# Adaptive-norm products of layer 0 on VectorE, mLSTM projections ahead of the state weights, and other tiles for layer 1's chunks

## The chip, the core and the metric

The kernel runs on one core of a Trainium2 chip. The metric is the device time of one execution in microseconds (us). Engines go by the profile's names: PE is TensorE (matmuls; PEld is its weight load), DVE is VectorE, ACT is ScalarE, POOL is GpSimd, SP is SyncE, whose queue issues the loads.

## What is computed

Two layers of a diffusion trunk over 256 latent and 256 context tokens, width 1024, float32. For this change three pieces of the reference matter.

```python
s_c, s_cc = jax.nn.silu(c), jax.nn.silu(c_ctx)
mod   = jnp.split((s_c @ w_ada[l] + b_ada[l])[:, None, :], 6, axis=-1)
mod_c = jnp.split(s_cc @ w_ada[l][:, :n_cm * D_MODEL] + b_ada[l][:n_cm * D_MODEL], n_cm)   # n_cm: 6 in layer 0, 2 in layer 1
h = modulate(rms_norm(x, g_norm1[l]), mod[0], mod[1])                # then h @ w_in[l] for four parallel mixers
# mixer B (mLSTM): q and k are silu(short_conv(h @ w_bq)), silu(short_conv(h @ w_bk));
# its stabiliser is a running sum and a running maximum over the tokens of the gate projections
x = x + mod[2] * (merge_branches(ya, yb, yc, yd) @ w_out[l])
x = x + mod[5] * squared_relu_mlp(modulate(rms_norm(x, g_norm2[l]), mod[3], mod[4]), w_ff1[l], w_ff2[l])
```

The modulation is a product of one row (or two rows, with the context's) with a 1024 x 6144 matrix: 24 MB a layer are read for very little arithmetic.

## The kernel before, in words

All weights are streamed once. A piece of weight is 128 x 1024 floats (512 KB): `_prep` loads it into a `raw` tile (three of these go round), ScalarE rounds it to `whi` (L136), VectorE takes the remainder `wlo` (L137), and a product is three TensorE passes over the high and low parts (L164 to L166, L193 to L195, L215 to L217). There are two `whi` and two `wlo` tiles, apart from some pieces that are kept longer, which take the four wide `w8` tiles (`wide`). The order of the pieces is a list, `specs`, made by the plan functions; `get` hands out the next piece and lets `_prep` run one piece ahead. Below this list a scheduler orders each engine's instructions by their place in the program and by when it reckons them ready; on the chip each engine then runs its list in order.

Between the pieces lie the chunks of the modulation matrix (`ada`): `plan` puts one behind each split piece while the list `fill` lasts. A chunk isn't split. Its load goes into a `raw` tile too, and right after the `get` of the piece before it `ada_chunk` uses it. Layer 0's first third of the matrix is done by another path at the start (`ada_start`, L529). Its other two thirds are 32 chunks (two groups g of 16, each of 8 rows k by two halves j), which follow the pieces of mixer A, its readout (RA), mixer B and the first merges (M0). For each of them TensorE runs four matmuls of 256 columns (L400) into the four 32-row bands of a PSUM tile that it holds through a whole group, with both conditioning vectors as the stationary operand; `ada_end` then copies, transposes and adds the bias.

Layer 1's 48 chunks (g 0 to 2) lie between the pieces of layer 0's feed-forward. These go to VectorE (`ada_vec`): each chunk is multiplied by a per-partition scalar and added to a 128 x 1024 accumulator in a `w4` tile (L360 for the first row, L362 for the others), once for each side, where group 0 has two sides (latent and context) and the others one. After eight chunks `ada_sum` adds the accumulator over the partitions with matmuls against a selector (L374), four for each side.

Mixer B (`mixer_b`): the gate projection (L215 to L217), its transpose, then on VectorE a chain of logarithm, running sums and running maxima on 36 rows (L783 to L817), which ends in a small diagonal matrix (`bdg`, L821). TensorE multiplies it with ones (L823), transposes U, and then projects k and q (four pieces, `bk`, `bq`, by `fm`, L164 to L166), each followed by a short convolution (`conv`, L749 to L757), and then v (`bv`, four pieces). State weights (L855) follow the projection of v.

Of the kernel before, what the change touches and what calls it, by code (L numbers as in the profile page):

```python
# [10 lines left out]
AF = mybir.ActivationFunctionType  # L11
ALU = mybir.AluOpType
# [5 lines left out]
TOK = CTX + LAT  # L18
KT = DM // 128
# [12 lines left out]
P_BADA, P_G1, P_G2 = 0, 96, 112  # L32
# [8 lines left out]
class Trunk:  # L41
# [63 lines left out]
    def _prep(self):  # L105
        nc = self.nc
        i = self.next_prep
        self.next_prep += 1
        key, parts, split, dest = self.specs[i]
        if key[0] == "ad" and key[1]:  # L110
            raw = self.t("w4", [128, 1024])
        else:
            raw = self.wp.tile([128, 1024], F32, name=f"raw{i}", tag="raw", bufs=self.wb)
# [226 lines left out]
    def ada_specs(self, l, g):  # L340
        w = self.io["w_ada"]
        out = []
        for k in range(KT):
            for j in range(2):
                c0 = g * 2048 + j * 1024
                out.append((("ada", l, g, k, j), [(w[l, k * 128:(k + 1) * 128, c0:c0 + 1024].rearrange("p (a c) -> p a c", a=1), (1, 1024))], False, None))
        return sorted(out, key=lambda o: o[0][4]) if l else out

    def ada_vec(self, key):

        nc = self.nc
        _, l, g, k, jj = key
        raw, _ = self.get(key)
        sides = (0, 1) if g == 0 else (0,)
        if k == 0:
            self.ada_acc = [self.t("w4", [128, 1024], name=f"aacc{g}{jj}{r}") for r in sides]
        for r in sides:
            acc, s = self.ada_acc[r], self.scol[:, k, r:r + 1]
# [30 lines left out]

    def ada_chunk(self, key):  # L390
        nc = self.nc
        _, l, g, k, jj = key
        if l:
            return self.ada_vec(key)
        raw, _ = self.get(key)
        if k == 0 and jj == 0:
            self.ada_ps = self.pd()
        for q in range(4):

            nc.tensor.matmul(self.ada_ps[32 * q:32 * q + 32, jj * 256:(jj + 1) * 256], self.scol[:, k, :], raw[:, q * 256:(q + 1) * 256],  # L400
                             start=(k == 0 and jj == 0), stop=(k == KT - 1), skip_group_check=True)
        if k == KT - 1 and jj == 1:
            self.ada_end(l, g, self.ada_ps)

    def ada_end(self, l, g, ps):
        nc = self.nc
        row = self.t("d2", [128, 512], name=f"arow{l}{g}")
        nc.scalar.activation(out=row, in_=ps, func=AF.Copy)
        pt = self.pm()
        for c in range(4):  # L410
            self.tr(pt[:, c * 128:(c + 1) * 128], row[:, c * 128:(c + 1) * 128])
        n0 = l * 48 + g * 16
        view = lambda ap: ap.rearrange("p (j q c) -> p j c q", j=2, q=4)
        bias = view(self.PT[:, P_BADA + n0:P_BADA + n0 + 16])
        for r in range(2):
            for jj in range(2):
                nc.vector.tensor_tensor(
                    out=view(self.MOD[l][:, g * 16:(g + 1) * 16, r])[:, jj],
                    in0=pt.rearrange("p (j c q s) -> p j c q s", j=2, c=2, q=4)[:, jj, :, :, r],
                    in1=bias[:, jj], op=ALU.add)  # L420
        self.ada_gs(l, g, (0, 1))
# [338 lines left out]
    def mixer_b(self, l):  # L760
# [59 lines left out]
        for a in range(2):  # L820
            nc.vector.tensor_scalar(out=dg[0:R, a, :], in0=self.ident[0:R, 0:R], scalar1=me[0:R, a:a + 1], scalar2=None, op0=ALU.mult)  # L821
        pe = self.pm()
# [15 lines left out]
        kT = [self.conv(l, 1, mt, self.fm(self.get(("bk", l, mt)), 0, TOK), 0, 0.125) for mt in range(2)]  # L838
        qT = [self.conv(l, 0, mt, self.fm(self.get(("bq", l, mt)), q0, TOK), q0, 1.0) for mt in range(2)]
# [698 lines left out]
```

## Time and profile before

| | us |
|---|---|
| median of 3 runs | 1850.93 (1849.62 to 1853.4) |
| the profiled execution, its own time | 1851.94 |
| span of its profile | 1850.2 |
| PE busy in it | 1805.8 (98%) |
| DVE busy | 1134.1 (61%) |
| ACT busy | 836.3 (45%) |
| granted TensorE clock, mean | 0.994 |

The profile is of one execution. Busy time is summed per engine over its instructions; a wait is the idle time of an engine just before an instruction, put down to what that instruction waited for last. A window row gives the busy time of each engine in a stretch, with the number of instructions in brackets, then the granted TensorE clock as a share of 2.4 GHz. Of TensorE, matmuls are pipelined: the distance from one start to the next tells the cost of one, not the duration that is shown.

### The profile page before, as it was taken

How to read it: one execution, taken by the hardware profiler on the slowest of the kernel's cores; microseconds unless marked ns; L12 is line 12 of the kernel's file. 1: busy time of each engine (PE TensorE's matmuls, PEld its weight loads, DVE VectorE, ACT ScalarE, POOL GpSimd, SP SyncE). 2: the span in 40 equal slices, each digit the busy share in tenths (PEclk: the TensorE clock that was granted, in tenths of full speed). 3: DMA queues.
4: the chain of work that ended last, by engine and by line, in shares of the span. 5: the costliest groups of instructions: out<-in, count | busy, mean ns of one | idle time of the engine just before them, and what ended most of it. 6: DMA issues, size and time to landing. Idle time of an engine off the chain costs nothing.

```text
span 1850.2 us, 28703 instructions
## 1 busy us (share of the span) xinstructions
PE 1805.8 (98%) x11414; PEld 1554.8 (84%) x11414; DVE 1134.1 (61%) x1983; ACT 836.3 (45%) x1487; POOL 123.1 (7%) x139
## 2 busy tenths in 40 slices
PE   7999999999999999999999999999999999989998
PEld 5888877799667778898777888988899979889998
DVE  5566654627754444557775665588665866566665
ACT  4343433434763333443333334444454774545555
POOL 0000000000001111010111000000000001001110
PEclk9999999999999999999999999999999999999999
DMA  9533343333112233315565655222234524544554
GB/s 288 180 92 100 117 149 117 112 109 91 46 35 69 68 126 114 114 45 159 164 192 179 192 183 159 72 69 69 81 118 150 160 68 138 159 149 148 183 183 137
DMA packets 222343, 235.26 MB, mean 127 GB/s; under 512 B 8320, under 2 KB 209408, under 8 KB 221952
## 3 DMA queue, kind: packets, MB, share of 16 engines
q1 hardware_dynamic: 222208, 233.42, 40.9%
q8 instruction: 90, 1.47, 0.3%
q14 instruction: 45, 0.37, 0.1%
HBM read 229.20 MB, written 4.19 MB: 126 GB/s over the span
## 4 chain that ended last, share of the span: by engine, by line
PE 81%; DVE 7%; DMA 6%; ACT 3%; issue 2%; SPq 0%; POOL 0%; ACTq 0%; DVEq 0%; POOLq 0%
PE pd L193 12%; PE pd L195 12%; PE pd L194 12%; DMA raw<-in_w_ada_dram 5%; PE pd L215 5%; PE pd L216 4%; PE pd L217 4%; PE pd L164 4%; PE pd L165 4%; PE pd L166 4%; PE pm L642 2%; PE pm L233 2%; DVE wlo L137 2%; PE pm L909 1%; PE pm L1100 1%
## 5 line engine op out<-in xcount | busy, mean ns | idle before, releaser
L137 DVE TENSOR_TENSOR wlo<-raw,whi 128x1024 fp32r<-128x1024 f32 x305 | 386.3, 1267 | 299.1 <-ACT whi L136 297.2
L136 ACT ACTIVATE whi<-raw 128x1024 fp32r<-128x1024 f32 x305 | 322.0, 1057 | 402.2 <-PE pd L194 171.8
L195 PE MATMUL pd<-HH,wlo 128*128 128x256 f32 (+1 forms) x1104 | 371.7, 337 | 8.8 <-DVE wlo L137 8.7
L193 PE MATMUL pd<-HH,whi 128*128 128x256 f32 (+1 forms) x1104 | 372.9, 338 | 1.2 <-ACT whi L136 1.2
L194 PE MATMUL pd<-HL,whi 128*128 128x256 f32 (+1 forms) x1104 | 371.5, 337 | 0.0
L195 PEld LDWEIGHTS pd<-HH,wlo 128*128 128x128 f32 x1104 | 210.0, 190 | 32.0 <-DVE wlo L137 11.8
L193 PEld LDWEIGHTS pd<-HH,whi 128*128 128x128 f32 x1104 | 209.9, 190 | 25.9 <-issue 3.9
L194 PEld LDWEIGHTS pd<-HL,whi 128*128 128x128 f32 x1104 | 209.9, 190 | 20.8 <-issue 0.7
L193 PE MATMUL pd<-b,whi 128*128 128x256 f32 (+1 forms) x528 | 175.5, 332 | 0.0
L195 PE MATMUL pd<-b,wlo 128*128 128x256 f32 (+1 forms) x528 | 175.2, 332 | 0.2 <-DVE wlo L137 0.2
L194 PE MATMUL pd<-b,whi 128*128 128x256 f32 (+1 forms) x528 | 175.3, 332 | 0.0
L215 PE MATMUL pd<-whi,HH 128*128 128x256 f32 x592 | 169.0, 286 | 0.0
L217 PE MATMUL pd<-wlo,HH 128*128 128x256 f32 x592 | 168.6, 285 | 0.0
L216 PE MATMUL pd<-whi,HL 128*128 128x256 f32 x592 | 168.0, 284 | 0.0
L215 PEld LDWEIGHTS pd<-whi,HH 128*128 128x128 f32 x592 | 113.4, 192 | 4.2 <-issue 4.1
L216 PEld LDWEIGHTS pd<-whi,HL 128*128 128x128 f32 x592 | 113.4, 192 | 0.3 <-issue 0.2
L217 PEld LDWEIGHTS pd<-wlo,HH 128*128 128x128 f32 x592 | 113.4, 192 | 0.2 <-issue 0.2
L362 DVE SCALAR_TENSOR_TENSOR aacc<-raw,scol,aacc 128x1024 f32<-128x1024 f32 x56 | 72.9, 1308 | 59.4 <-DMA raw<-in_w_ada_dram 59.2
L193 PEld LDWEIGHTS pd<-b,whi 128*128 128x128 f32 x528 | 100.3, 190 | 10.5 <-issue 0.8
L195 PEld LDWEIGHTS pd<-b,wlo 128*128 128x128 f32 x528 | 100.3, 190 | 10.2 <-DVE wlo L137 0.9
L194 PEld LDWEIGHTS pd<-b,whi 128*128 128x128 f32 x528 | 100.3, 190 | 9.3
L437 ACT ACTIVATE w<-X 128x256 f32<-128x256 f32 x120 | 48.1, 413 | 128.9 <-DVE X L1257 128.9
(419 smaller groups left out, 3312.3 us busy)
## 6 DMA issues: line engine op xcount, KB each, us to landing
raw<-in_w_in_dram SPq DMA_DIRECT2D x148, 512.0 KB, 3.5
raw<-in_w_ff_dram SPq DMA_DIRECT2D x128, 512.0 KB, 3.9
raw<-in_w_ada_dram SPq DMA_DIRECT2D x80, 512.0 KB, 4.0
raw<-in_w_branch_dram SPq DMA_DIRECT2D x24, 512.0 KB, 3.4
raw<-in_w_out_dram SPq DMA_DIRECT2D x16, 512.0 KB, 3.4
w<-in_w_ada_dram SPq DMA_DIRECT2D x28, 256.0 KB, 5.5
raw<-in_w_branch_dram SPq DMA_DIRECT2D x16, 256.0 KB, 4.0
spill<-X SPq DMA_DIRECT2D x1, 2048.0 KB, 8.6
```

Source lines behind the costliest of these rows:

```text
L136: nc.scalar.activation(out=hi[:, 0:n], in_=raw[:, 0:n], func=AF.Copy)
L137: nc.vector.tensor_tensor(out=lo[:, 0:n], in0=raw[:, 0:n], in1=hi[:, 0:n].bitcast(F32), op=ALU.subtract)
L164: nc.tensor.matmul(out, lh, rh, start=(i == 0), stop=False)
L165: nc.tensor.matmul(out, lh, rl, start=False, stop=False)
L166: nc.tensor.matmul(out, ll, rh, start=False, stop=(i == n - 1))
L193: nc.tensor.matmul(o, wh, act[0], start=(k == 0), stop=False, skip_group_check=True)
L194: nc.tensor.matmul(o, wh, act[1], start=False, stop=False, skip_group_check=True)
L195: nc.tensor.matmul(o, wl, act[0], start=False, stop=(k == KT - 1), skip_group_check=True)
L215: nc.tensor.matmul(o, hh, wh, start=first, stop=False, skip_group_check=True)
L216: nc.tensor.matmul(o, hl, wh, start=False, stop=False, skip_group_check=True)
L217: nc.tensor.matmul(o, hh, wl, start=False, stop=last, skip_group_check=True)
L362: nc.vector.scalar_tensor_tensor(out=acc, in0=raw, scalar=s, in1=acc, op0=ALU.mult, op1=ALU.add)
```

## The change

Three things are changed.

1. Layer 0's 32 chunks go the way of layer 1's: VectorE multiplies and accumulates, for both sides, and `ada_sum` closes each half group; the TensorE path with `ada_end` is gone. The chunks of layer 0 are sorted by half, as layer 1's are.
2. In both layers, mixer B's four projections of k and q with their convolutions stand before the matmul L823 in the program.
3. The chunks of layer 1 are loaded into `w8` tiles (four, the size of two chunks each) and no longer into `raw` tiles.

```diff
@@ _prep
         if key[0] == "ad" and key[1]:
             raw = self.t("w4", [128, 1024])
+        elif key[0] == "ada" and key[1]:
+            raw = self.t("w8", [128, 1024])
         else:
             raw = self.wp.tile([128, 1024], F32, name=f"raw{i}", tag="raw", bufs=self.wb)
@@ ada_specs
-        return sorted(out, key=lambda o: o[0][4]) if l else out
+        return sorted(out, key=lambda o: o[0][4])
-    def ada_vec(self, key):
+    def ada_chunk(self, key):
         nc = self.nc
         _, l, g, k, jj = key
         raw, _ = self.get(key)
-        sides = (0, 1) if g == 0 else (0,)
+        sides = (0, 1) if l == 0 or g == 0 else (0,)
...
-    def ada_chunk(self, key):
-        nc = self.nc
-        _, l, g, k, jj = key
-        if l:
-            return self.ada_vec(key)
-        raw, _ = self.get(key)
-        if k == 0 and jj == 0:
-            self.ada_ps = self.pd()
-        for q in range(4):
-            nc.tensor.matmul(self.ada_ps[32 * q:32 * q + 32, jj * 256:(jj + 1) * 256], self.scol[:, k, :], raw[:, q * 256:(q + 1) * 256],
-                             start=(k == 0 and jj == 0), stop=(k == KT - 1), skip_group_check=True)
-        if k == KT - 1 and jj == 1:
-            self.ada_end(l, g, self.ada_ps)
-    def ada_end(self, l, g, ps):
...
@@ mixer_b
             nc.vector.tensor_scalar(out=dg[0:R, a, :], ...)
+        kT = [self.conv(l, 1, mt, self.fm(self.get(("bk", l, mt)), 0, TOK), 0, 0.125) for mt in range(2)]
+        qT = [self.conv(l, 0, mt, self.fm(self.get(("bq", l, mt)), q0, TOK), q0, 1.0) for mt in range(2)]
         pe = self.pm()
         nc.tensor.matmul(pe[:, 0:72], self.ones[0:R, :], dg[0:R].rearrange("p a b -> p (a b)"), start=True, stop=True)
...
         nc.scalar.activation(out=wk, in_=wk, func=AF.Exp)
-        kT = [self.conv(l, 1, mt, self.fm(self.get(("bk", l, mt)), 0, TOK), 0, 0.125) for mt in range(2)]
-        qT = [self.conv(l, 0, mt, self.fm(self.get(("bq", l, mt)), q0, TOK), q0, 1.0) for mt in range(2)]
         V = self.t("w8", [128, 4, 4, 129], name=f"bv{l}")
```

## Rows read from the trace of the kernel before

**Rows 1.** The page's first part: busy time, share and instructions of each engine.
```profile
PE 1805.8 (98%) x11414; PEld 1554.8 (84%) x11414; DVE 1134.1 (61%) x1983; ACT 836.3 (45%) x1487; POOL 123.1 (7%) x139
```
**Rows 2.** Windows of layer 0's chunk stretch (length; busy PE, PEld, DVE, ACT, POOL; clock; DMA).
```profile
72.00:205.00 133.00, 132.57 (x889) 109.18 (x888) 89.47 (x149) 51.96 (x83) 1.64 (x4) 1.00 0.32 96
205.00:286.00 81.00, 78.60 (x580) 65.58 (x580) 48.81 (x82) 35.78 (x53) 0.53 (x1) 1.00 0.47 145
286.00:364.00 78.00, 78.00 (x449) 58.58 (x446) 42.91 (x114) 30.60 (x71) 2.44 (x8) 1.00 0.34 107
```
**Rows 3.** Waits of PE from 840 to 1135 us, then of the span (total, times, longest).
```profile
PE pd L195 <- DVE wlo L137: 8.0, 6, 3.1
...
PE pm L823 <- DVE bdg L821: 5.9, 2, 3.5
```
**Rows 4.** Timeline of PE around one chunk of layer 0 (start, duration, engine, line).
```profile
104.69 0.39 PE L165 MATMUL pd<-HL,whi 128*128 128x512 f32 x1
104.92 0.40 PE L166 MATMUL pd<-HH,wlo 128*128 128x512 f32 x1
105.24 0.64 PE L400 MATMUL pd<-raw,scol 128*32 128x256 f32 x8
105.81 0.50 PE L164 MATMUL pd<-HH,whi 128*128 128x512 f32 x1
106.15 0.39 PE L165 MATMUL pd<-HL,whi 128*128 128x512 f32 x1
```
**Rows 5.** The same windows as rows 2, L400 alone (busy PE, PEld with counts).
```profile
72.00:205.00 133.00, 10.12 (x96) 2.41 (x96) 1.00 0.32 96
205.00:286.00 81.00, 8.89 (x96) 2.15 (x96) 1.00 0.47 145
286.00:364.00 78.00, 5.11 (x64) 1.26 (x64) 1.00 0.34 107
```
**Rows 6.** Timeline of PE around one sum of layer 1, two sides.
```profile
893.61 0.39 PE L195 MATMUL pd<-HH,wlo 128*128 128x512 f32 x1
893.93 1.07 PE L374 MATMUL pm<-aacc,selr 128*32 128x256 f32 x16
894.93 0.50 PE L193 MATMUL pd<-HH,whi 128*128 128x512 f32 x1
```
**Rows 7.** Lines L360 and L362 (minimum/median/maximum ns), and L362's group on the page.
```profile
L360 DVE TENSOR_SCALAR aacc<-raw,scol x8: 748/752/754, 833.7 to 1071.1; 128x1024 f32<-128x1024 f32 x8
L362 DVE SCALAR_TENSOR_TENSOR aacc<-raw,scol,aacc x56: 1271/1285/1916, 840.8 to 1111.8; 128x1024 f32<-128x1024 f32 x56
L362 DVE SCALAR_TENSOR_TENSOR aacc<-raw,scol,aacc 128x1024 f32<-128x1024 f32 x56 | 72.9, 1308 | 59.4 <-DMA raw<-in_w_ada_dram 59.2
```
**Rows 8.** Windows: a head of layer 1's mixer A, and the feed-forward of layer 0.
```profile
1206.00:1228.00 22.00, 22.00 (x129) 18.16 (x128) 18.69 (x41) 10.41 (x19) 0.00 (x0) 1.00 0.30 85
840.00:865.00 25.00, 25.00 (x112) 20.71 (x111) 20.26 (x24) 8.51 (x13) 1.49 (x1) 1.00 0.52 155
```
**Rows 9.** Waits of DVE in 840 to 865 us (total, times, longest).
```profile
DVE aacc L362 <- DMA raw<-in_w_ada_dram: 3.0, 3, 1.4
```
**Rows 10.** Windows of mixer B in layer 1, and line L855.
```profile
1307.00:1311.00 4.00, 0.54 (x3) 0.19 (x2) 3.71 (x11) 0.47 (x1) 0.00 (x0) 0.87 0.41 130
1311.00:1317.00 6.00, 6.00 (x27) 5.67 (x27) 3.88 (x6) 4.38 (x8) 0.00 (x0) 0.52 0.19 59
...
L855 DVE TENSOR_TENSOR w<-pm,bwk x8: 414/416/425, 283.7 to 1345.3; 128x256 f32<-128x256 f32 x8
```
**Rows 11.** Timelines of DVE and PE in the feed-forward at 912 us.
```profile
912.52 1.28 DVE L362 SCALAR_TENSOR_TENSOR aacc<-raw,scol,aacc 128x1024 f32<-128x1024 f32 x1 [3.85 <-DMA raw<-in_w_ada_dram]
913.73 1.22 DVE L137 TENSOR_TENSOR wlo<-raw,whi 128x1024 fp32r<-128x1024 f32 x1
...
915.00 0.50 PE L195 MATMUL pd<-HH,wlo 128*128 128x512 f32 x1 [2.30 <-DVE wlo L137]
```
**Rows 12.** Window behind the longest stall of the feed-forward.
```profile
1006.00:1010.00 4.00, 4.00 (x12) 3.09 (x11) 1.23 (x2) 0.26 (x1) 0.00 (x0) 0.57 0.97 332
```

More of the change, by code (lines that the diff above doesn't have):

```diff
@@ L388, in ada_sum @@
                 self.ada_gs(l, g, sides)
-    def ada_chunk(self, key):
-        nc = self.nc
-        _, l, g, k, jj = key
-        if l:
-            return self.ada_vec(key)
-        raw, _ = self.get(key)
-        if k == 0 and jj == 0:
-            self.ada_ps = self.pd()
-        for q in range(4):
-            nc.tensor.matmul(self.ada_ps[32 * q:32 * q + 32, jj * 256:(jj + 1) * 256], self.scol[:, k, :], raw[:, q * 256:(q + 1) * 256],
-                             start=(k == 0 and jj == 0), stop=(k == KT - 1), skip_group_check=True)
-        if k == KT - 1 and jj == 1:
-            self.ada_end(l, g, self.ada_ps)
-    def ada_end(self, l, g, ps):
[L406 to L421, printed above, removed]
     def ada_gs(self, l, g, sides):
```

## The prediction

> **What bounds the kernel now.** I read the engines' totals first [rows 1]: TensorE is busy for 98% of the span, VectorE for 61%. So time can be won only where TensorE does less or waits less, and lost only where it waits more. The windows come next [rows 2]. In the stretch with layer 0's chunks (72 to 364 us) TensorE is busy for 289.2 of 292 us, while VectorE's busy time by windows is 89.47, 48.81 and 42.91, in all 181.2 us. The reader is to see that TensorE sets the pace there and that VectorE has room, but not the same room in each window. Then the waits [rows 3]: TensorE stands 8.0 us for the low parts of weights (`wlo`) in layer 0's feed-forward, 6 times, and 5.9 us for `bdg` in mixer B, twice in the span. Each part of the change touches one of these: TensorE's work in 72 to 364 us, the wait of L823, and the wait for `wlo` in the feed-forward.
>
> **Part 1, layer 0's chunks: what goes.** From one matmul of 512 columns to the next lie 0.23 us, start to start (104.69 to 104.92 [rows 4]). Around a chunk it is 0.32 ahead of L400, 0.57 for its four matmuls (eight records), and 0.34 behind. Less the two distances of 0.23 that are there anyway, a chunk costs 0.09 + 0.57 + 0.11 = 0.77 us. The records per window are 96, 96 and 64 [rows 5], so 12, 12 and 8 chunks, and TensorE loses 32 x 0.77 = 24.6 us of work.
>
> A page prices this otherwise: by the Trainium skill, FP8 and Floating Point Precision, TensorE Precision Notes, true float32 takes four passes; as an estimate from that and 2.4 GHz, four matmuls of 256 columns would be 1.7 us and the 32 chunks 55 us. The row has 0.57 us for the four, which lie in four separate bands of 32 columns, and the row decides.
>
> **What comes.** Four sums, one after each eight chunks, each as the two-sided one of layer 1 [rows 6]: 1.00 us and the same 0.2 around it, 4.8 us (one of them in the first window, two in the second, one in the third). The transposes stay eight; in four groups where there were two they add two such switches, 0.4 us, left to the range. TensorE's balance is -19.8 us. On VectorE each chunk is two instructions: 8 of 64 at 0.752 us and 56 at 1.285 us [rows 7], 78.0 us, 2.44 us a chunk. Loads are the same in number and size on SP's queue. What changes there is when a `raw` tile comes free: so far after TensorE's 0.57 us, then after VectorE's two instructions, and a load of the next piece waits behind that on SP.
>
> **Where VectorE stops hiding it.** With the chunks its busy time is 89.5 + 29.3 = 118.8 in the first window (133 us), 48.8 + 29.3 = 78.1 in the second (81 us) and 42.9 + 19.5 = 62.4 in the third (78 us). TensorE alone would need 133 - 9.2 + 1.2 = 125.0, 81 - 9.2 + 2.4 - 2.4 = 71.8 (with part 2's wait gone) and 78 - 6.2 + 1.2 = 73.0. So VectorE becomes the limit in the first two windows unless it can be kept busy without a break. How far it can be is nowhere shown for this mixture. Two rows bound it [rows 8]: a head of layer 1's mixer A, a chain through three engines, has it busy for 18.69 of 22.00 us, 0.85, with TensorE full; and 840 to 865 us, chunks among other work, for 20.26 of 25 us of which 3.0 went on chunk loads [rows 9], so 0.92 of the time that was left, with TensorE at 25.00 of 25.00. I take 0.92, since a chunk's instructions wait for their load alone and can lie in the gaps of the chains, as they do in that row. Then the windows become 118.8/0.92 = 129.1 (-3.9), 78.1/0.92 = 84.9 (+3.9) and 73.0 (-5.0, TensorE still the limit): -5 us. I give back 1 us for chunk loads that come late as in the feed-forward (59.2 us of waits there over 56 instructions [rows 7], but with 48 chunks from 833.7 to 1111.8 us, 5.8 apart; here they are 81/12 = 6.8 to 133/12 = 11 apart). Part 1 with the first wait of part 2: **-4 us**. Its ends: 0.85 throughout gives 139.8, 91.9 and 73.4, that is +13; TensorE the limit throughout gives 125.0 + 71.8 + 73.0 = 269.8, that is -22.
>
> **Part 2, mixer B.** L823 waits 3.5 us in layer 1 and, by the difference, 2.4 in layer 0 [rows 3]. In layer 0 that is inside the second window and counted above. In layer 1 the wait has a tail: 1307 to 1311 us has 0.54 us of matmuls, and 1311 to 1317 us runs at a granted clock of 0.52 [rows 10], the lower level of 1.2 GHz, so about 2.9 of these 6 us are lost. Together 6.4. After the change the four projections stand ahead of L823 and cover the chain: two of them already ran ahead of it, the other two bring 48 matmuls more. What queues behind: L823, the transposes of U, and the weights up to L855, which runs until 1345.3 in layer 1, 34 us behind the end of the wait; four v pieces lie between, so they can be some 6 us later for nothing. On VectorE the remainders of the two q pieces now fall into the scan chain (1.22 us each), and the convolutions come behind it, so the first PSUM tile for v may be late by about 1 us. I take **-5 us**; the ends are -6.4, and +3 if TensorE waits for a q piece's `wlo` about as long as it waited for `bdg`.
>
> **Part 3, the feed-forward.** One stall shows them all [rows 11]: VectorE stands 3.85 us before a chunk's instruction for its load, the `wlo` behind it is late, and TensorE waits. A load can only be issued when one of three `raw` tiles, shared with the weights, is free. With four tiles of their own, chunks can be loaded further ahead, and the weights keep all three. The stalls are 8.0 us [rows 3], and behind the longest one 1006 to 1010 us runs at a clock of 0.57 [rows 12], another 1.7 us: 9.7. No work is added. What is late next is VectorE itself, with 20.26 busy and 3.0 waiting of 25 us in 840 to 865 [rows 8, 9], so I keep back a quarter: **-7 us**, between 0 and -9.7.
>
> **Sum.** -4 - 5 - 7 = -16 us on the profiled execution's 1851.9, so 1835.9. It lies 1.0 above the median of the runs, to which the forecast refers: **1835 us**. The rivals' times are put on the median in the same way.
>
> **Rivals.** *VectorE becomes the bound of layer 0's mixers* (the slower side). Place: 72 to 286 us. At 0.85 the three parts sum to +13 - 5 - 7 = +1 (1852); at 0.80 the windows are 148.5, 97.6 and 78.0, +32, so +20 (1871). It decides from 0.85 down, which is what the head of layer 1 shows. For it: 78.1 us of work in the 81 of the second window, and `raw` tiles that now wait for VectorE, so a late chunk also holds up the next weight's load. Against it: VectorE idles for 292 - 181 = 111 us of the stretch [rows 2], and 78 us that wait for nothing but loads can go into these gaps.
> [...]
>
> *TensorE stays the bound everywhere*: -22 - 6.4 - 9.7 = -38, 1813. For it: the chunk instructions could fill waits that exist anyway. Against: it needs 0.95 and more of VectorE in the first window and over 1 in the second, unless work slips into the third.
>
> *The new tiles don't help*: the `w8` tiles are held by other work (the wide pieces at the start of the feed-forward) or VectorE, not the load, was late: -4 - 5 = -9, 1842. Against: chunks are worked on from 833.7 us on [rows 7], so the early pieces are then done, and the stalls shown lie later [rows 11, 12].
>
> *A q piece is late in mixer B*: -4 + 3 - 7 = -8, 1843.
>
> **Chances and numbers.** Forecast 0.41; VectorE the bound 0.26 (0.17 of it slower, 0.07 within, 0.02 faster); TensorE the bound 0.17; no help from the tiles 0.10; a late q piece 0.06. A difference of 0.2%, 3.7 us, is about what a measurement of this kernel can tell. Within it I count 0.07 and 0.01 each of three other cases; so faster 0.73, within 0.10, slower 0.17. The forecast's own range is 1824 to 1846. The range for 8 in 10 runs from 1814, near the case with TensorE as the bound, to 1857, some way into the case of VectorE.
>
> **What would show it.** In the profile after: no L400; in layer 0, 64 records of L374 more, 56 of L362 and 8 of L360. VectorE busy near 92% in the window that held mixer A's readout and mixer B, with TensorE waiting for `wlo` there; no wait of L823 and no clock of 0.5 in layer 1's mixer B; waits of L362 for loads in the feed-forward down from 59 us to a few, and TensorE's waits for `wlo` there under 3 us. I am wrong if the stretch to the first merges gets longer than 292 us, if L362's waits stay in the feed-forward, or if a wait for `wlo` takes the place of `bdg`.

## The result and the profile after

The changed kernel takes **1831.28 us** (median of 4 runs, 1830.24 to 1832.05) where the kernel before, beside it, takes 1852.16. The ratio is 0.9885 with a 95% interval of 0.9867 to 0.9903, so it is 1.15% faster. The forecast was 1835 and its range 1814 to 1857. The profiled execution has a span of 1829.0 us, 21.2 less than before.

In the changed kernel lines have moved: the old L137 (`wlo`) is L140, L136 (`whi`) L139, L193 to L195 are L196 to L198, L164 to L166 L167 to L169, L215 to L217 L218 to L220, L360 and L362 L363 and L365, L374 L377, L823 L796, L821 L791, L855 L826.

The first part of the page, against [rows 1]:

```profile
PE 1785.1 (98%) x11222; PEld 1553.7 (85%) x11222; DVE 1201.7 (66%) x2047; ACT 835.8 (46%) x1489; POOL 122.7 (7%) x139
```

TensorE has 192 instructions less, the 256 of L400 out and 64 of the sums in, and 20.7 us less busy time (the forecast's balance was -19.8). VectorE has 64 instructions and 67.6 us more.

The next question is where along the span the time went. The table gives the start of some landmarks on TensorE in both traces and the difference, after less before.

| landmark | before | after | difference |
|---|---|---|---|
| layer 0: first product of mixer A (`ah`) | 76.63 | 76.82 | +0.2 |
| last product with mixer A's state (`aS`) | 203.97 | 205.20 | +1.2 |
| transposes of mixer B's gates (`Gp`) | 226.55 | 225.37 | -1.2 |
| `bdg` | 242.71 | 245.53 | +2.8 |
| first product of mixer B's state (`bv`) | 284.64 | 277.06 | -7.6 |
| transposes of mixer B's readout (`bh`) | 455.79 | 443.68 | -12.1 |
| feed-forward, first product | 798.16 | 786.02 | -12.1 |
| layer 1: first product of mixer A's pieces | 1169.65 | 1150.42 | -19.2 |
| `Gp` | 1296.31 | 1277.08 | -19.2 |
| first product of mixer B's state (`bv`) | 1344.76 | 1325.01 | -19.8 |
| layer 1's feed-forward, last product with the wide pieces at its start | 1667.67 | 1646.53 | -21.1 |
| last transposes | 1843.31 | 1822.17 | -21.1 |

Three stages tell the story: layer 0's mixers give 12.3 us (the forecast had 4), the feed-forward 7.1 (7), and mixer B in layer 1 gives 0.5 (5). The 1.4 us between mixer B's first state product in layer 1 and the start of layer 1's feed-forward belong to no part of the change, and their cause stays open.

**Layer 0's mixers.** The same windows as [rows 2], and the stretch to 352 us, which is where the old 364 now lies (columns as there):

```profile
72.00:205.00 133.00, 128.77 (x842) 114.59 (x841) 121.81 (x179) 52.20 (x81) 1.11 (x3) 0.99 0.40 114
205.00:286.00 81.00, 75.57 (x521) 66.27 (x520) 68.75 (x108) 37.19 (x60) 1.05 (x2) 0.98 0.40 120
...
72.00:352.00 280.00, 270.34 (x1705) 233.74 (x1704) 243.64 (x402) 115.99 (x202) 4.61 (x13) 0.99 0.41 119
```

VectorE is at 121.81/133 = 0.92 in the first window, the share that I had assumed, and at 0.85 in the second; over the stretch it is 243.64/280 = 0.87. Layer 0's mixers by landmarks: mixer A from its first product to its last state product is 1.0 us longer than before, from there to mixer B's first state product it is 8.8 us less, and from there to `bh` 4.5 us less. The second window is less full than I had reckoned (68.75 us and not 78.1) because the chunks did not stay in their windows: of the 62 chunk instructions from 72 us on, 30 run in the first window and 18 in the second, where I had put 24 and 24.

TensorE lost 9 us in waits, most of them within 20 us, in the last head of mixer A and the beginning of its readout. The timeline of TensorE there, the rows with a wait:

```profile
194.98 1.16 PE L612 MATMUL pm<-ah 128*128 128x128 f32 x8 [1.55 <-ACT ah L608]
197.62 2.07 PE L621 MATMUL pm<-ah 128*128 128x128 f32 x8 [1.48 <-DVE ah L634]
201.64 1.16 PE L652 MATMUL pm<-av,w 128*128 128x128 f32 x8 [0.69 <-ACT w L648]
208.65 0.44 PE L236 MATMUL pm<-cst,arow 128*128 128x128 f32 x2 [2.18 <-ACT arow L380]
210.52 0.39 PE L218 MATMUL pd<-whi,HH 128*128 128x256 f32 x1 [1.43 <-DVE d L689]
```

These five are 7.3 us; two waits for `wlo` in mixer B (at 239.6 and 248.2 us) add 1.7. Before, the only wait in this stretch was the 2.4 us for `bdg`. VectorE's timeline beside it shows why:

```profile
196.27 0.69 DVE L630 TENSOR_TENSOR ah<-ah 128x512 f32<-128x512 f32 x1
196.87 0.69 DVE L634 TENSOR_TENSOR ah<-ah 128x512 f32<-128x512 f32 x1
...
198.17 1.28 DVE L365 SCALAR_TENSOR_TENSOR aacc<-raw,scol,aacc 128x1024 f32<-128x1024 f32 x1
...
200.16 2.48 DVE L365 SCALAR_TENSOR_TENSOR aacc<-raw,scol,aacc 128x1024 f32<-128x1024 f32 x2
206.60 0.75 DVE L363 TENSOR_SCALAR aacc<-raw,scol 128x1024 f32<-128x1024 f32 x1 [3.96 <-PE pm L377]
207.27 2.46 DVE L674 TENSOR_REDUCE ssq<-w 128x4 f32<-128x512 f32 x4
```

The chunk products (L365) stand between the steps of the head's chain (L630, L634). Then the first product of the next group (L363) waits 3.96 us for an accumulator tile that the sum's matmuls (L377) have still to read, and the readout's reductions (L674) wait behind it on the same queue. This is the first of the four sums, over the half group whose last product ended at 124.1 us; it stands behind mixer A's products on TensorE's queue and starts at 205.41, 81 us later. No run moves it forward, so what that would give back stays open. The granted clock falls there as well; the windows of the two halves:

```profile
172.00:197.00 25.00, 22.46 (x180) 21.53 (x178) 22.84 (x34) 8.56 (x12) 0.00 (x0) 1.00 0.33 94
197.00:216.00 19.00, 13.94 (x95) 12.24 (x96) 14.98 (x26) 9.38 (x16) 1.57 (x3) 0.82 0.38 110
```

The mean clock of 0.82 is two spells at the lower level of 1.2 GHz, of some 3.4 us each (from 197.6 and from 211.1 us).

**The feed-forward.** The waits of TensorE from 833 to 1120 us, against 8.0 us in 6 waits in [rows 3]:

```profile
PE pd L198 <- DVE wlo L140: 1.7, 2, 1.4
```

The window of [rows 8] that has chunks among other work:

```profile
840.00:865.00 25.00, 25.00 (x109) 20.27 (x110) 25.00 (x33) 7.31 (x13) 0.00 (x0) 1.00 0.73 230
```

And line L365 in the whole span, with what its engine stood idle for, against L362 in [rows 7]; the tile `w` is the new `w8` tile:

```profile
L365 DVE SCALAR_TENSOR_TENSOR aacc<-raw,scol,aacc x56: 1157/1278/1299, 71.4 to 339.6; 128x1024 f32<-128x1024 f32 x56
L365 DVE SCALAR_TENSOR_TENSOR aacc<-w,scol,aacc x56: 1267/1280/2097, 812.4 to 964.7; 128x1024 f32<-128x1024 f32 x56
...
  DMA w<-in_w_ada_dram: 6.3, 3
```

Waits for chunk loads fell from 59.2 to 6.3 us, VectorE is busy for 25.00 of 25 us where it was for 20.26, and layer 1's chunks are through at 965 us, not at 1112. The fall of the clock at 1006 us [rows 12] is gone.

**Mixer B in layer 1.** The timeline of TensorE around `bdg`, the rows with a wait and one behind them:

```profile
1292.74 0.41 PE L796 MATMUL pm<-bdg,ones 36*128 36x72 f32 x2 [1.28 <-DVE bdg L791]
1293.46 0.63 PE L236 MATMUL pm<-cst,w 128*128 128x128 f32 x4 [0.31 <-DVE w L782]
1294.64 0.30 PE L236 MATMUL pm<-cst,w 128*128 128x128 f32 x1 [0.56 <-DVE w L727]
...
1295.57 0.39 PE L218 MATMUL pd<-whi,HH 128*128 128x256 f32 x1 [0.39 <-ACT whi L139]
...
1297.18 0.58 PE L169 MATMUL pd<-HH,wlo 128*128 128x256 f32 x1 [1.11 <-DVE wlo L140]
1297.56 0.42 PE L167 MATMUL pd<-HH,whi 128*128 128x256 f32 x1
```

One wait of 3.5 us became five of 3.65 us together, and the clock falls again (1296.7 to 1300.1 us at the lower level; 256 columns take 0.21 us there from one start to the next, 1297.78 to 1297.99, and 0.12 ahead of the waits, 1291.06 to 1291.18). ScalarE's timeline in the same microseconds says what is late:

```profile
1283.93 0.67 ACT L719 ACTIVATE w<-pd,PT 128x512 f32<-128x512 f32 x1
1290.18 1.28 ACT L725 ACT_TABLE_LOAD   x1 [5.58 <-DVE w L723]
1291.47 0.63 ACT L725 ACTIVATE w<-w 128x512 f32<-128x512 f32 x1
...
1293.52 1.99 ACT L139 ACTIVATE whi<-raw 128x1024 fp32r<-128x1024 f32 x2
```

The Tanh of the first convolution (L725) now stands early in ScalarE's queue, and waits 5.58 us for VectorE's part of the convolution (L723), which is itself scheduled between the scans. The rounding of the last q piece (L139) stands behind it and runs at 1293.52, so the last of the four projections, which was to help cover the wait for `bdg`, is not ready when `bdg` is late; the other three are through by then (TensorE's last product ahead of the wait starts at 1291.18).

### The profile page after: what moved, and what is told of

It is laid out like the page before. It is cut to its first block, busy times and chain, and to the rows that moved or that the text cites. A ratio compares the mean times of both kernels' runs of the same rounds, so it can differ in the third digit from the quotient of the medians.

```text
span 1829.0 us, 28369 instructions
## 1 busy us (share of the span) xinstructions
PE 1785.1 (98%) x11222; PEld 1553.7 (85%) x11222; DVE 1201.7 (66%) x2047; ACT 835.8 (46%) x1489; POOL 122.7 (7%) x139
## 4 chain that ended last, share of the span: by engine, by line
PE 85%; DVE 7%; ACT 3%; issue 2%; DMA 2%; SPq 0%; POOL 0%; ACTq 0%; DVEq 0%; POOLq 0%
PE pd L198 14%; PE pd L196 14%; PE pd L197 14%; PE pd L218 4%; PE pd L220 4%; PE pd L219 4%; PE pd L167 4%; PE pd L169 4%; PE pd L168 4%; PE pm L236 2%; PE pm L612 2%; DVE wlo L140 2%; PE pm L880 1%; PE pm L1071 1%; PE pm L1175 1%
## 5 line engine op out<-in xcount | busy, mean ns | idle before, releaser
L140 DVE TENSOR_TENSOR wlo<-raw,whi 128x1024 fp32r<-128x1024 f32 x305 | 385.6, 1264 | 288.3 <-ACT whi L139 286.3
L139 ACT ACTIVATE whi<-raw 128x1024 fp32r<-128x1024 f32 x305 | 322.0, 1057 | 420.8 <-PE pd L197 174.0
L198 PE MATMUL pd<-HH,wlo 128*128 128x256 f32 (+1 forms) x1104 | 370.4, 336 | 3.0 <-DVE wlo L140 2.8
L196 PE MATMUL pd<-HH,whi 128*128 128x256 f32 (+1 forms) x1104 | 371.8, 337 | 0.2 <-ACT whi L139 0.2
L198 PEld LDWEIGHTS pd<-HH,wlo 128*128 128x128 f32 x1104 | 209.6, 190 | 25.3 <-DVE wlo L140 4.8
L196 PEld LDWEIGHTS pd<-HH,whi 128*128 128x128 f32 x1104 | 209.5, 190 | 22.6 <-issue 1.6
L198 PE MATMUL pd<-b,wlo 128*128 128x256 f32 (+1 forms) x528 | 175.3, 332 | 0.4 <-DVE wlo L140 0.4
L196 PE MATMUL pd<-b,whi 128*128 128x256 f32 (+1 forms) x528 | 175.6, 333 | 0.0
L218 PE MATMUL pd<-whi,HH 128*128 128x256 f32 x592 | 169.1, 286 | 2.0 <-DVE d L689 1.4
L220 PE MATMUL pd<-wlo,HH 128*128 128x256 f32 x592 | 169.8, 287 | 0.0
L218 PEld LDWEIGHTS pd<-whi,HH 128*128 128x128 f32 x592 | 114.2, 193 | 3.2 <-DVE d L689 1.7
L220 PEld LDWEIGHTS pd<-wlo,HH 128*128 128x128 f32 x592 | 114.1, 193 | 0.2 <-issue 0.2
L198 PEld LDWEIGHTS pd<-b,wlo 128*128 128x128 f32 x528 | 100.3, 190 | 10.9 <-DVE wlo L140 1.6
L196 PEld LDWEIGHTS pd<-b,whi 128*128 128x128 f32 x528 | 100.3, 190 | 10.5 <-issue 0.8
L1221 POOL TENSOR_TENSOR mg<-mg,d 128x512 f32<-128x512 f32 (+1 forms) x48 | 54.0, 1128 | 580.2 <-DVE d L1220 458.7
```

What stands on the lines that cost most here:

```text
L139: nc.scalar.activation(out=hi[:, 0:n], in_=raw[:, 0:n], func=AF.Copy)
L140: nc.vector.tensor_tensor(out=lo[:, 0:n], in0=raw[:, 0:n], in1=hi[:, 0:n].bitcast(F32), op=ALU.subtract)
L196: nc.tensor.matmul(o, wh, act[0], start=(k == 0), stop=False, skip_group_check=True)
L198: nc.tensor.matmul(o, wl, act[0], start=False, stop=(k == KT - 1), skip_group_check=True)
L218: nc.tensor.matmul(o, hh, wh, start=first, stop=False, skip_group_check=True)
L220: nc.tensor.matmul(o, hh, wl, start=False, stop=last, skip_group_check=True)
```

## The experiments

My theory after the result, S: VectorE sets the pace of layer 0's mixers in places, not throughout, so part 1 gives about half of what TensorE saves; part 2 gives next to nothing, because waits on other queues replace the one removed; part 3 gives its 7. Its rivals stand in the expectations. Each run is timed against the kernel before on its own chip; the medians of before were 1851.53 for the first four, 1852.58 for the next four and 1853.13 for the last four. In the rows below the line numbers are those of each run's own kernel.

| run | median | ratio to before (95%) |
|---|---|---|
| changed kernel | 1831.28 | 0.9885 (0.9867 to 0.9903) |
| 1, part 3 alone | 1844.19 | 0.9957 (0.9942 to 0.9972) |
| 2, part 2 alone | 1849.57 | 0.9989 (0.9980 to 0.9999) |
| 3, part 1 alone | 1841.41 | 0.9945 (0.9929 to 0.9962) |
| 4, parts 1 and 3 | 1832.15 | 0.9895 (0.9881 to 0.9910) |
| 5, chunks for one side | 1825.11 | 0.9853 (0.9836 to 0.9869) |
| 6, convolutions behind | 1838.82 | 0.9929 (0.9913 to 0.9945) |
| 7, no chunks behind the readout | 1840.80 | 0.9935 (0.9920 to 0.9950) |
| 8, 6 and 7 together | 1847.28 | 0.9972 (0.9961 to 0.9983) |
| 9, own room for C | 1834.40 | 0.9898 (0.9883 to 0.9912) |
| 10, 7 with own room for C | 1842.05 | 0.9945 (0.9930 to 0.9960) |
| 11, part 2 in layer 0 only | 1829.92 | 0.9875 (0.9859 to 0.9891) |
| 12, q rounded ahead in layer 1 | 1827.86 | 0.9865 (0.9851 to 0.9880) |

### Each part alone

**Run 1.** The kernel before with the new tiles only:

```diff
+        elif key[0] == "ada" and key[1]:
+            raw = self.t("w8", [128, 1024])
```

> Edit: part 3 alone, layer 1's chunks in w8 tiles, in the kernel before. Theory S (the gain is a sum by stage: layer 0's mixers about -12, mixer B of layer 1 about 0, the feed-forward about -7): 7 us less than the kernel before, TensorE's waits for wlo in layer 0's feed-forward from 8.0 us to under 3, the waits of the chunk instructions for their loads from 59 us to under 10. Rival R (the whole gain is the 20 us of TensorE work taken away, the other parts do nothing): within 2 us of the kernel before.

Measured: -7.3 us. TensorE's waits for `wlo` in the feed-forward are 1.6 us, as in the changed kernel. Part 3 is what it was taken for.

**Run 2.** The kernel before with the two lines `kT` and `qT` moved ahead of the `bdg` matmul, as in the change.

> Edit: part 2 alone, the four projections of mixer B ahead of the matmul with bdg, in the kernel before. Theory S: 0 to 3 us less than before. In layer 1 the time from the transposes of the gates to the first matmul of v stays near 24 us (23.96 before), because ScalarE stands at the convolution's Tanh, which waits for VectorE's scan chain, and the rounding of the last q piece is queued behind it. The forecast's own term says -6 to -9: both waits of bdg (5.9 us) and the half clock behind the second are gone.

Measured: -2.0 us, with an interval from -3.7 to -0.2 (0.9980 and 0.9999 of 1851.5). In its trace layer 0 has no wait left from 72 to 364 us, which agrees with the 2.4 us forecast there. In layer 1 the stage gives 0.2 us; its waits of TensorE from 1250 to 1345 us:

```profile
PE pm L825 <- DVE bdg L821: 1.3, 1, 1.3
PE pd L166 <- DVE wlo L137: 0.8, 1, 0.8
PE pm L233 <- DVE w L757: 0.6, 1, 0.6
PE pm L233 <- DVE w L812: 0.3, 1, 0.3
...
```

The wait of 3.5 us has come back as four, 3.0 us together, without any chunk on VectorE in this stretch. So part 1 is not the cause.

**Run 3.** The kernel before with the chunks on VectorE only: the `l == 0` branch of `ada_chunk` and `ada_end` removed, and

```diff
-        sides = (0, 1) if g == 0 else (0,)
+        sides = (0, 1) if l == 0 or g == 0 else (0,)
```

> Edit: part 1 alone, layer 0's chunks on VectorE, in the kernel before. Theory S: 5 to 10 us less than before, since without the early projections VectorE's scan chain, now with chunk instructions in it, keeps TensorE waiting at the matmul with bdg for longer than the 2.4 us of before (5 us or more). Rival R: 19 to 20 us less, the work of TensorE that is gone.

Measured: -10.1 us. Its waits of TensorE from 72 to 364 us:

```profile
PE pm L791 <- DVE bdg L788: 3.2, 1, 3.2
PE pm L233 <- ACT arow L377: 2.2, 1, 2.2
PE pm L609 <- ACT ah L605: 1.5, 1, 1.5
PE pm L618 <- DVE ah L631: 1.5, 1, 1.5
...
```

The stall at the end of mixer A comes with part 1 alone, and the wait for `bdg` grows from 2.4 to 3.2 us. S had 5 to 10, the rival 19 to 20: by the time it is S, at its upper end. S's reason was off: it had put 5 us or more on the wait for `bdg`, and the larger part of the loss is the stall at the end of mixer A.

**Run 4.** The changed kernel with part 2 undone.

> Edit: parts 1 and 3 without part 2. Theory S: e3's gain and 7 us more, so 12 to 17 less than before, 4 to 9 more than the changed kernel; all of that difference in layer 0's mixer B, none in layer 1's. Rival R: as the changed kernel, within 2 us.

Measured: 1832.15, a ratio of 0.9895 against the changed kernel's 0.9885. Here S fell and the rival held: on top of parts 1 and 3, part 2 is worth 1 to 2 us (0.9 by the medians, 1.9 by the ratios, whose intervals overlap), not 4 to 9. In the traces layer 0's stage from `Gp` to the first state product is 51.7 us in the changed kernel and 55.1 here, so the gain there is 3.4; in layer 1 the stage is 47.3 us here and 47.9 in the changed kernel. Parts 1 and 3 together give -19.4 where each alone gives -7.3 and -10.1, and the whole change -20.9: the parts nearly add up, and part 2 is the small one.

### What limits layer 0's mixers

**Run 5.** The changed kernel with layer 0's chunks for the latent side only; the context side takes the same modulation. That is the part of the computation that is left out; it removes 32 of VectorE's chunk instructions, half the matmuls of each sum, and one of the two accumulator tiles of each half group.

```diff
-        sides = (0, 1) if l == 0 or g == 0 else (0,)
+        sides = (0, 1) if l and g == 0 else (0,)
```

> Edit: the changed kernel with layer 0's chunks multiplied for the latent side alone; the context side's modulation of the last two thirds is a copy of the latent one (left out: its products, half of VectorE's chunk work, 39 us, and half of the sums on TensorE, 2 us). Theory V (VectorE's occupancy sets the stretch of layer 0's chunks, which lies some 10 us above TensorE's own need): 8 to 12 us less than the changed kernel, the waits around the end of mixer A gone. Rival (TensorE's work is the limit there already): 1 to 3 us less, for the sums.

Measured: 1825.11, by the ratios 0.0032 x 1852 = 5.9 us below the changed kernel, between the two expectations. Some 2 us of it are TensorE's (four sums of 1.00 us halved [rows 6]). The window that held the stall:

```profile
197.00:216.00 19.00, 17.49 (x150) 16.60 (x149) 15.49 (x25) 12.70 (x20) 1.58 (x3) 1.00 0.21 60
```

With less to do on VectorE the waits in the last head go, TensorE is busy for 17.49 us there and not for 13.94, and the clock stays at 1.00. The loads are the same in both, so it is VectorE's added work that makes the stall in the head. Behind the head this run doesn't tell causes apart: the sums are shorter as well (the 2.18 us for the sum's row, `arow`, are gone), with one accumulator tile for each half group L363 no longer waits for a tile, and the wait for `d` (L689) stays, at 1.51 us. By the trace of one execution the stretch from mixer A's first product to `bh` is 8.0 us shorter (358.9 against 366.9): 2 for the sums, and TensorE is idle for 4.8 us there where it was for 9.7, with no spell at the lower clock. So half of the 78 us added costs some 4 us by the totals and some 6 by this trace. VectorE's work costs time in places; it doesn't set the pace of the whole stretch.

**Run 6.** The changed kernel with the four projections where the change put them, and the convolutions behind `wk`, where they were:

```diff
-        kT = [self.conv(l, 1, mt, self.fm(self.get(("bk", l, mt)), 0, TOK), 0, 0.125) for mt in range(2)]
-        qT = [self.conv(l, 0, mt, self.fm(self.get(("bq", l, mt)), q0, TOK), q0, 1.0) for mt in range(2)]
+        pk4 = [self.fm(self.get(("bk", l, mt)), 0, TOK) for mt in range(2)]
+        pq4 = [self.fm(self.get(("bq", l, mt)), q0, TOK) for mt in range(2)]
```

> Edit: the changed kernel with the four projections ahead of the matmul with bdg, but their convolutions behind the weights wk, where they stood before. Theory Q (the convolution's Tanh stands on ScalarE waiting for VectorE's scan chain, and the rounding of the last q piece waits behind it): TensorE finds its pieces, layer 1's time from the gate transposes to the first matmul of v goes from 24 us to 19 to 21, and the kernel is 3 to 6 us faster than the changed one. Rival (the scan chain itself sets the time, wherever the convolutions stand): within 1.5 us of the changed kernel.

Measured: 1838.82, about 8 us slower than the changed kernel (0.9929 against 0.9885), which nobody expected. The only wait of TensorE from 225 to 300 us, in layer 0:

```profile
PE pd L218 <- DVE w L723: 7.4, 1, 7.4
```

The four unread projections hold all four tiles of the PSUM ring `pd`, and v's projection waits 7.4 us until the first convolution (L723) has read one. With four tiles in this ring the convolutions have to stand early, because they release them. The price is what run 2 and the changed kernel show: their Tanh stands early on ScalarE. In layer 1, which theory Q was about, the stage from `Gp` to the first state product takes 51.0 us and not less than the changed kernel's 47.9, with waits of 2.9 us for `bEM`, 1.5 for `whi` and 0.8 for `wlo`.

**Run 7.** The changed kernel without chunks behind the four pieces of mixer A's readout, so that the stall at its end has less on VectorE:

```diff
-        if fill and split and self.fill:
+        if fill and split and self.fill and key[0] != "ag":
```

> Edit: the changed kernel with no chunk behind the four pieces of mixer A's readout (and none in layer 1's, which has none anyway), so that the chunks behind them lie four pieces later. Theory V: the stall of some 9 us and two falls of the clock at the end of mixer A come from VectorE being full there; they shrink, 3 to 8 us less than the changed kernel. Rival (work only slides: VectorE is as full in the merges that take the four chunks): within 2 us.

Measured: 1840.80, about 9 us slower. The last state product of mixer A is 5.3 us earlier, as hoped (199.91 against 205.20), but of this 1.0 is left at `Gp` (224.41 against 225.37), and from there to the readout of mixer B the kernel loses 13 (`bh` at 455.70, +12.0). The window in which most of it goes:

```profile
350.00:370.00 20.00, 14.65 (x74) 10.67 (x75) 16.91 (x30) 8.89 (x17) 0.00 (x0) 0.83 0.51 158
```

VectorE's first product of the last half group (L363) starts only at 355 us, after a wait for a tile. I read this as a want of accumulator tiles, since mixer B's state C holds one of the four `w4` tiles by then; runs 9 and 10 test that.

**Run 8.** The edits of runs 6 and 7 together.

> Edit: e6 and e7 together. Theories Q and V: the sum of both, 6 to 14 us less than the changed kernel. If one of the two does nothing, as the other alone.

Measured: 1847.28, 16 us slower than the changed kernel. The two losses add up (8 and 9).

**Run 9.** The changed kernel with C in a room of its own; two rings of small scratch tiles are one tile shorter to make room.

```diff
-        C = self.t("w4", [128, 2, 2, 129], name=f"C{l}")
+        C = self.sm([128, 2, 2, 129], "bC", 1)
```

> The changed kernel with mixer B's state C in a room of its own, so that all four accumulator tiles are free for the chunks through the merges (two scratch rings of the small tiles are one tile shorter to make the room). Theory V (VectorE sets the pace of layer 0's mixers, and it loses time only where an accumulator tile is not free): in the changed kernel those waits, 4.7 us, lie at 193 to 209 us, ahead of C, and the last half group is nearly through when C is made, so the time is within 2 us of the changed kernel's 1831. Rival: the tile that C holds delays the merges here too, and the time falls by 4 us or more.

Measured: 1834.40. By the ratios it is 2.4 us above the changed kernel, with intervals that overlap: a little outside the 2 us expected, and nothing of the 4 us gain that the rival wanted. C's tile does not hold up the changed kernel, unless the shorter rings, which no run has by themselves, cost as much as it gives.

**Run 10.** Run 7 with the same room for C.

> The run without chunks behind the readout's pieces (1840.8 us) again, with C in a room of its own. Theory V and my reading of that run: the end of mixer A stays about 5 us earlier, and the merges no longer lose 13 us, because the last half group of chunks has its two accumulator tiles: 1824 to 1830 us. Rival: the merges lose because the half group is late in itself, with too little VectorE time left before the modulation is needed or too few loads under way: 1836 us or more, with the waits in 350 to 370 us as before.

Measured: 1842.05, no better than run 7: my reading of it falls. L363 waits for no tile any more, and yet the stretch loses the same. TensorE's timeline from 350 to 370 us, the rows with a wait and the sum behind them:

```profile
357.80 0.77 PE L880 MATMUL pm<-bv,w 128*128 128x129 f32 x2 [3.78 <-DVE w L862]
...
363.08 0.80 PE L880 MATMUL pm<-bv,w 128*128 128x129 f32 x2 [2.36 <-DVE w L862]
...
366.74 1.06 PE L377 MATMUL pm<-aacc,selr 128*32 128x256 f32 x14
368.30 0.44 PE L236 MATMUL pm<-cst,arow 128*128 128x128 f32 x2 [0.49 <-ACT arow L380]
```

The last chunk product (L365) starts at 363.7 us, so the last sum (L377) runs from 363.8 to 369 us, and the next products (L218, the projections for mixers C and D, which follow the merges) come behind it on TensorE's queue, at 369.22. From 353 us until then TensorE has nothing but the sum and the last products of mixer B (L850, L880), a chain that waits for VectorE while VectorE has chunks in between. In the changed kernel the last chunk product starts at 339.6 us and the sum at 362.62, when its inputs are long ready and matmuls of those projections stand on both sides of it; from 296 to 456 us no window shows TensorE idle. So by this trace the cost is that the last chunks come late and the projections are ordered behind their sum. I did not move the sum by itself, so that is argued from the timeline and not shown by a run.

### What limits mixer B in layer 1

**Run 11.** The changed kernel with the projections moved in layer 0 only (`if l == 0` at the new place, `if l` at the old one).

> The changed kernel with mixer B's projections moved in layer 0 alone; layer 1 has the old order. Theory Q (in layer 1 the move gives nothing, because the wait for bdg comes back as waits behind ScalarE's queue and one more clock fall): within 1.5 us of the changed kernel's 1831, layer 1's stretch from the gate transposes to v's first product 24 us as before. Rival (my forecast): 4 to 6 us slower than the changed kernel.

Measured: 1829.92, ratio 0.9875: the same as the changed kernel. The old wait is back at its full size in layer 1, as TensorE's timeline shows,

```profile
1291.56 0.41 PE L797 MATMUL pm<-bdg,ones 36*128 36x72 f32 x2 [3.46 <-DVE bdg L791]
```

and the stage from `Gp` to the first state product is 1324.36 - 1277.02 = 47.3 us, against 47.9 in the changed kernel and 48.4 before. So in layer 1 part 2 gives nothing, and what little part 2 brings lies in layer 0, where this run has the projections ahead and takes 51.9 us for the stage.

**Run 12.** The changed kernel with layer 1's two q pieces rounded into `w8` tiles ahead of the first convolution:

```diff
-                self.plan((nm, l, mt), [self.win(l, o + 128 * mt, 128)])
+                self.plan((nm, l, mt), [self.win(l, o + 128 * mt, 128)], dest=self.wide if l and nm == "bq" else None)
...
+        self.look = 3 if l else 1
         kT = [self.conv(l, 1, mt, self.fm(self.get(("bk", l, mt)), 0, TOK), 0, 0.125) for mt in range(2)]
+        self.look = 1
```

> The changed kernel with the two q pieces of layer 1 rounded into tiles of their own ahead of the first convolution, so that their rounding on ScalarE no longer stands behind the convolution's Tanh. Theory Q: TensorE then projects q while VectorE is in the scans, the wait for bdg and the clock fall at 1296.7 us go, and the stretch from layer 1's gate transposes to v's first product falls from 24 us to 19 to 21: 1827 to 1829 us. Rival: the scan chain on VectorE sets that stretch whatever TensorE has to do beside it, v's product waits for PSUM tiles or for weights instead, and the time is within 1 us of 1831.

Measured: 1827.86, ratio 0.9865. That is inside theory Q's 1827 to 1829, and the lowest of all kernels here that compute everything, but its interval overlaps that of the changed kernel. The trace bears it out: from `Gp` to the first state product it takes 1321.43 - 1275.99 = 45.4 us, 2.5 less than in the changed kernel. TensorE's waits from 1290 to 1330 us, and below them the windows from `Gp` to v's products and of the wait:

```profile
PE pm L798 <- DVE bdg L791: 2.8, 1, 2.8
PE pm L236 <- DVE w L782: 0.4, 1, 0.4
```

```profile
1276.00:1297.10 21.10, 17.89 (x108) 15.68 (x107) 16.89 (x28) 11.56 (x15) 0.13 (x1) 1.00 0.42 125
1293.00:1297.00 4.00, 0.79 (x6) 0.60 (x6) 3.78 (x10) 0.86 (x2) 0.00 (x0) 1.00 0.46 131
```

The theory is half right. All four projections now run before `bdg`, no wait for `wlo` or `whi` is left behind it, and the clock stays at 1.00. But the wait for `bdg` did not go: it is 2.8 us, since the projections run without a break and are through before the scans are. The scans are later, too: L798 with `bdg` starts 19.9 us behind `Gp`, against 15.7 for the same matmul in the changed kernel and 14.5 in run 11. ScalarE's timeline shows most of it:

```profile
1281.93 1.06 ACT L139 ACTIVATE whi<-raw 128x1024 fp32r<-128x1024 f32 x1 [1.60 <-PE pd L168]
1283.01 1.28 ACT L757 ACT_TABLE_LOAD   x1
1284.31 0.72 ACT L757 ACTIVATE w<-w,ones 36x512 f32<-36x512 f32 x1
```

The logarithm of the scan chain (L757) now stands behind the rounding of a weight, which waits for TensorE, and starts 8.3 us behind `Gp`; in the changed kernel it started after 4.0 (1281.11), and such a rounding followed it (1282.96). So the edit that freed the q pieces delayed the chain on the same queue. The gain is that the q work now lies ahead of the wait instead of in pieces behind it, at full clock. The stretch from `Gp` to v's first product is 1297.11 - 1275.99 = 21.1 us, at the upper end of the 19 to 21 that theory Q expected.

## Why the prediction was right, and where its steps were not

**The total** is 21 us where the forecast had 16, on the right side and inside the range, but two of the three terms were wrong, in opposite directions: -12 for -4, about 0 for the -5, and -7 for -7. That the total came within 5 us is in part luck.

**Part 1, TensorE's side: right.** The balance of -19.8 us is the -20.7 of the page's busy time, so the 0.57 us of [rows 4] was the right price. The estimate of 55 us for the 32 chunks, worked out from the four passes that the FP8 and Floating Point Precision page of the Trainium skill gives for true float32 (TensorE Precision Notes), has nothing like it in the trace.

**Part 1, VectorE's side: mis-sized.** The step that failed is "the windows become 118.8/0.92 = 129.1 (-3.9), 78.1/0.92 = 84.9 (+3.9) and 73.0 (-5.0, TensorE still the limit)". By the landmarks at the windows' ends the changes were +1.0, -8.8 and -4.5. The 0.92 held where VectorE was fullest, in the first window; in the one that held mixer A's readout and mixer B, where I had looked for it, it was 0.85. What failed was to give each window its own fixed share of chunks and to let the second pay +3.9: chunk work came forward into the first window (30 instructions for 24), so the first gained nothing and the second got shorter. The same numbers over the whole stretch, (181.2 + 78.0)/0.92 = 281.7 us, give -10, and the trace gave 279.7 (-12.3); that these lie so near is luck, since VectorE was at 0.87 over the stretch and not at 0.92. TensorE alone would have needed 269.8. The 10 us between are no general slowness of VectorE; they are idle time of TensorE (280 - 270.34 = 9.7 us), 9 of it the waits shown above, while the spells at the lower clock lie in its busy time. Run 5 ties the waits in the last head to VectorE's added work. One cost was left out: I had let a chunk's instructions "wait for their load alone", and L363 waited 4.7 us, in two waits, for accumulator tiles that L377 had still to read. The sums, of which I had put one into the first window, all ran behind it (at 205.41, 236.86, 295.74 and 362.62 us).

**The rival "VectorE the bound", "decides from 0.85 down": wrong as a rule.** VectorE came out at 0.85 in the second window and 0.87 over the stretch, and the kernel was 12 us faster there. I had read 0.85 as a ceiling; it was only the share that the work needed. The Trainium skill (Perfetto Trace Analysis, Identifying the Most-Contended Engine) takes occupancy for VectorE, judges TensorE's headroom by its share of the peak arithmetic and its weight loads and not by its matmul busy time, and calls the engine that comes out highest the most contended. Here that is VectorE, at 0.87 against 233.74/280 = 0.83 of weight loads. That ranking agrees with run 5, where taking VectorE's work away helped. It doesn't say whether the stretch is longer or shorter than before; it was 12.3 us shorter.

**Part 1, late loads: right and small.** The chunks in layer 0 waited 1.5 us in 4 waits for their loads; I had given 1.

**Part 2, layer 0: right.** The wait of 2.4 us is gone in run 2 and in the changed kernel, and the stage is shorter by 3.4 us than in run 4.

**Part 2, layer 1: wrong.** The step that failed is "the four projections stand ahead of L823 and cover the chain". I had counted what the q pieces bring to VectorE ("the remainders of the two q pieces now fall into the scan chain"), but not what the earlier convolution does to ScalarE's queue: its Tanh waits 5.58 us for VectorE, and the last q piece's rounding stands behind it. So `bdg` is still waited for (1.28 us), the last q piece's `wlo` among others takes the place of the rest (1.11), and the clock falls as before; these were signs of being wrong that I had named. It was my rival "a q piece is late in mixer B" that came true, on another queue than I thought, at about 0 instead of +3; I gave it 0.06. Run 11 shows the move in layer 1 to be worth nothing, run 12 that a rounding ahead of the Tanh gives 2.5 us of it in the trace, and run 6 that the convolutions cannot simply go behind.

**Part 3: right.** The forecast of -7 was met by -7.1 in the table and by -7.3 in run 1. Loads that come in time cut L365's waits from 59.2 to 6.3 us and TensorE's for `wlo` from 8.0 to 1.7, both as I said they would show. No run separates the two things that the tiles do, loading chunks further ahead and leaving the `raw` tiles to the weights.

## What to carry to other kernels

When work moves to an engine that has room, size it over the whole stretch that it can slide in, and then look for the chain through that engine with nothing beside it, for there the loss fell here. When a step is moved ahead of a wait, list what each in-order queue now has early, and ask for every entry what it waits for and what stands behind it; here the wait came back on the queue that was not looked at, and in run 12 the same queue made the chain itself later. A fix that takes work away from one stall can push it to another place: look where its last piece, and what is ordered behind that piece, will land.

## What the runs showed that was not expected

- A full ring of PSUM tiles cost more than the wait that the early projections were to hide: 7.4 us in run 6, against 2.4 us for `bdg` in layer 0 before.
- A wait at the same place does not always come with a fall of the clock. Before, 3.46 us for `bdg` in layer 1 was followed by a granted clock of 0.52 over 6 us [rows 10]; in run 12 a wait of 2.8 us at the same place, with 0.79 us of matmuls in 4 us, left it at 1.00.
- A VectorE at 25.00 of 25 us for a whole window did not slow TensorE beside it (25.00 of 25 at a clock of 1.00, 840 to 865 us), while at 22.84 of 25 us in 172 to 197 us, toward the end of mixer A, TensorE waited (22.46). I read from this that how full VectorE is says less than whether TensorE has other work beside the chain; no run varies that by itself.
